# Turning the 32x32 blocks in VectorE's transposes instead of in ScalarE's copies, in a hybrid decoder trunk

## The chip, the cores and the metric

One core of a Trainium2 chip runs the whole program. The metric is the device time of one execution in microseconds; the kernel before takes 1524.26 us (median of 3 runs, 1524.03 to 1524.69).

## What is computed

Two layers over 512 prompt tokens and 64 sample tokens (8 sequences of 8) that share all weights: a pooling mixer and then a gated delta-net mixer, each followed by a SwiGLU feed-forward block, with RMS norms around each. All is float32. The part that matters here is the delta rule of the second mixer, cut to its core:

```python
kb = k * beta[..., None]
a_mat = jnp.where(strict, jnp.einsum('bhnid,bhnjd->bhnij', kb, k) * decay, 0.0)
t_mat = a_mat + jnp.eye(CHUNK, dtype=jnp.float32)
solve = functools.partial(lax.linalg.triangular_solve, left_side=True, lower=True,
                          unit_diagonal=True)
u = solve(t_mat, v * beta[..., None])
w = solve(t_mat, kb * jnp.exp(gc)[..., None])
```

Each head needs the inverse of unit triangular matrices `t_mat`. The kernel works with 128x128 matrices, of a head and a span of 128 tokens: 16 heads in 4 groups of 4, 4 spans, so 16 matrices a group.

## The kernel before, in words

**Stages.** The pooling mixer and the first feed-forward block come first, then the delta-net mixer (about 440 to 1000 us of the profile), then the second feed-forward block. Large products are made of three fp32r matmuls each (`mm3`): weights and activations are split into a rounded part and the rest (`wh`, `wl`, `hH`, `hL`), the rounded part by ScalarE, the rest by VectorE or GpSimd. Products of the delta rule on attention-like matrices are plain fp32 matmuls.

**The delta-net part.** It goes by groups of 4 heads. `project` makes the next group's projections (`ps_m` in PSUM, which ScalarE evicts to `u` or `zz`) and short convolutions (`ac`), while `core` (line 1845) does the delta rule of the present one. `core` writes the group's 16 matrices into `Uw` (128 partitions x 16 x 128), inverts their diagonal 32x32 blocks with `inv32` (line 1348), and then combines the blocks by matmuls (`ps_k<-T,Uw`, `ps_s<-Uw,Rs` and so on) with ScalarE copying results back into `Uw`.

**`inv32`.** Four blocks of 32 sit on the diagonal of each of the 16 matrices, so 64 blocks of 32x32 a group. Per quarter of the partitions, ScalarE copies the diagonal blocks out of `Uw` into the compact tile `D32`, half of the tile `ii` (a "front copy": 32 partitions x 16 matrices x 32 columns, 4 a group). In before the compact tile is ordered column first, matrix second, so that the copy writes contiguously 16 matrices' elements of one column and reads them 128 elements apart. VectorE transposes 32x32 squares of it into `A` (tile `ia`, 1024 elements a partition, each of them from `D32` repeated twice). 31 elimination steps follow, two VectorE operations each. Then VectorE transposes the result back into `D32`, and four more ScalarE copies (the "back copies") put it into the diagonal blocks of `Uw`, again with the order of the two inner dimensions turned. Names in the profile: `ii<-Uw` are the front copies, `ia<-ii` is the first transpose, `ii<-ii` the second (a STREAM_TRANSPOSE), `Uw<-ii` the back copies.

**The order of the work.** Nothing runs in the order in which it is written. Each call on an engine is recorded with a price (`Plan.cost`) and its dependences; `Plan.finish` then draws an order for all five queues by list scheduling with priorities, and refines the priorities window by window by numbers from a table, `CHOSEN`, that were found for this program beforehand. The order so drawn is what the chip gets; each engine takes its queue strictly in that order. The prices that matter here: ScalarE pays by the number of elements, VectorE's transpose by whether all its inner dimensions have step one ("flat"):

```python
        if eng == "ACT":
            extra = 93 * sum(self.is_ap(k.get(w)) for w in ("scale", "bias")) + (100 if "accum_out" in k else 0)
            t = 0.833 * max(n, 16) + (170 if ps else 205) + extra
            return t - 102, t
...
        if method == "transpose":
            flat = all(list(x.ap)[-1][0] == 1 for x in ins + [out])
            t = 1.27 * n + 50 if flat else 1.95 * n + 80
```

Where the planner leaves PE idle for long, it can put in a matmul of ones (`ps_w`) that fills the time. All instructions recorded this way carry one line in the profile, L471, so that rows are told apart by tile names. An element of a PSUM ring is reused only when its reader is done: `ps_m` has two banks, so a projection's matmuls wait when ScalarE is late with an eviction.

Of the kernel before, what the change touches and what calls it, by code (L numbers as in the profile page):

```python
# [20 lines left out]
P = 128  # L21
# [36 lines left out]
class Plan:  # L58
# [22 lines left out]
        "0: 1309 22695 62500 86149 76489 52345 11844 46362 86704 95002 35544 99175 66637 4282 17667 3769 58400 "  # L81
        "43626 61818 54108 98212 3351 36664 80504 27809 72224 29735 64917 23111 41727; 1: 49023 63007 16460 16433 "
        "48491 76138 74771 74114 65160 87426 17314 27044 28440 98688 51496 33718 593 1426; 2: 23373 59272 95208 "
        "89396 40366 27552 29680 19213 96021 18743 91102 85125 83403 91744 68462 45573 19331 18226 28408 16995 "
        "68187 22777 99797 41955 91122 61703; 3: 40396; 4: 67260 44319 57030; 5: 95301 46915 67764; 8: 83208 "
        "18345; 10: 99903 85569 22644 7666 75444 7917; 12: 59185 64395 62859 17333 99370 79611 45665 40125 66046; "
        "13: 94477 22197 77279 9674 64267 65493 96055 75041 73772 26094 59228 59668 29996 66590 85309; 14: 83042 "
        "12131 52755 11078 68435 7966 75550 43253 125 86835 85075 55755 62104 79190 42298 15154 45791; 15: 13478 "
        "99481 73642 25401 41010 41421 4472 94786 57263 70338 23457 86193 45351 1546 40 98196 4967 43483; 16: "
        "93817 89234 40602 94462 17450 57861 22756 50039 37491 70807 55020 62920 18061 28656 38897 47689 31571 "  # L90
        "48068 27422 61755 69394 54039 64619 42263 70100; 17: 33665 21486 9197 46860 52000 86161 59917; 18: 20924 "
        "43334 44329 81674 7114 17045 25962 66993 50082 96718 92807 12531 16023 18431 40440 24596 71944 21112 "
        "74829 68196 92347 31561 74253 3392 53332 92281 2151 99102; 19: 36174 31947 59659 69612 29455 87315 54537 "
        "65141 74338 82015 79392 19887 11167 92294 51046 68011 40758; 20: 97279 69020 2370 45304 28726 5480 85426 "
        "12019 40119 96999 10385 72026 34446 22404; 21: 70291 28702 739 31944 70903 1060 42873 31326 30516 12342 "
        "60990 51629 93117 93896 40802 48208 18456 19228 57064 4679 59610 21243 54322 22912 89277 28893 62715 "
        "60621 92572 61631; 22: 13485 22541 37816 52495 66992 95880 36259 78259 30823 9512 66230 80373; 23: 61483 "
        "44103 90015 42044 24735 32849 41632 1074 64956 20942 94616 72706 60830 42378 30741 90719 93544 81412 "
        "40715 53278 39455 89612 15442 43550 39219 57896 7747; 24: 25348 67719 13180 61748 88090 95516 85975 5084 "
        "92478 83615 56195 82259 69748 62427 65712 91857 26297 40732 78694 27404 53404 22318 67031 71586 6132; "  # L100
        "25: 76647 39712 2771 66343 14209 23210 97810 92132 78974 59399 25063 67858 21491 50489 62995 15236; 26: "
        "79626 36368 19214 80387 56401 35576 82717 60375 53873; 27: 21984 71594 50907 14377 32244 15901 41074 "
        "39715 28392 20799 74780 83699 61252 83397 7982 32598 99600 98403 4570 27483 22362 4823 2508; 28: 24551 "
        "98160 24793 94220 95277 24650 68875 45170 18708 59416 15825 86583 66687 11861 95570 58210 99313 97019; "
        "29: 85578 28888 61342 95415 75453 40719 32701 86064 81345 14893 68856 50949 85498 13575 51784 91952 "
        "27692 26008 40138 57302 3814 97612 4449 36357 22750 70909 28219 7818 28047; 30: 86054 60496 97999 69673 "
        "50610 25685 50210; 31: 74073 13115 29407 43294 58203 62386 60992 80895 97830 46726 88271 52280 70227 "
        "37935 45598 50679 82011 34563 64041 61743 56793 56266 28529 89658 56010 55213 38050 60174 94562 29310; "
        "32: 16887 16469 35631 32010 42196 69810 20338 57949 56793 9113 36835 10599 67930 73391 67445 89104 59334 "
        "10750 4354 31147 20157 21006 12454 24106 89881 81438 8886 66266 40719 99502; 33: 95295 91479 81844 39720 "  # L110
        "25951 85067 56132 25492 97663 47361 15928 80071 51459 54484 10833 17494 29033 31355 68865 10887 35990 "
        "5777 79080 89337 9764 76787; 34: 95089 63681 56199 59606 75724 79194 18810 42081 81189 51667 19488 51936 "
        "59115 4849 50732 93986 68335 96897 92514 31139 17828 30084 75477 789 82272 1621 74838 6441 14529 49710; "
        "35: 76201 60413 56949 82903 33174 54908 54426 49959 77520 99541 55443 56649 3401 80937 48261 52653 75001 "
        "63908 97280 79647 8351 98108 52226 14386 80233 7388 14686 29780; 36: 10839 81171 71314 53994 76242 86866 "
        "63984 70449 2577 95749 86944 93238 65312; 37: 33496 69024 75456 28597 71266 19980; 38: 24426 13066; 39: "
        "89400; 40: 42141; 41: 94909; 42: 72179; 43: 15012; 44: 19665 41475; 45: 90900 90312 85593; 47: 55533 "
        "59254 30957 68731; 48: 15838 ",
        "0: 25782 39795 26872 58963 96576 71590 57680 53529 3102 48534 72061 49705 6781 35832 91582 33069 50362 "
        "71108 33270 39184 13549 78972 45267 39225 2455 79100 17756 80269 12399 57409; 1: 46402 13382 59970 83415 "  # L120
        "14691 65163 44574 31472 34406 49161 12567 48273 66815 46533 18979; 2: 58040 13854 16950 54319 59560 "
        "16016 14965 7900 15237 90384 17027 79128; 3: 32401 47644 98719 63000 17976 69867 14151 42123 34927; 4: "
        "18661 97896 5163 42810 82890 14811 23796; 5: 6334 83049; 6: 6739; 7: 23073; 9: 27471 98644; 11: 78001; "
        "12: 34315 65271; 13: 23776 35070 5091 11421 17100 1203 8855; 14: 98971; 15: 61486 53284 63025 8383 6639 "
        "11331 62257 66892 82335 74223 26226 95867 59421; 16: 86166 76125 78281 27438 26729 41349 50987 18963 "
        "60114 75460 99525 42303 33029 86092 45319 53211 36241 77822 4554 51767 28255 52396 83151 21072 13812 "
        "92609 81561 50211 70654 98; 17: 23599 20302 3092 43937 52212 18247 56370 87394 16459 19578 8608 37160 "
        "57650 85260 31716 31832 97582 42879 62691 40643 31202 26562 64599 48393 14029 46348 44616 29960 88973 "
        "50291; 18: 30583 75810 48361 88631 26459 70970 52092 19211 31704 50319 80529 51246 71427 45060 25577 "
        "23134; 19: 31080 29136 81033 55723 40922 16359 72123 56616 2311 22281 53256 33100; 20: 44142 76207 5248 "  # L130
        "94534 38694 75978 77463 67624 7305 4227 3834 94400 7416 66904 14979 26203 48624 45889 78506 40677 47535 "
        "89571 39981 6928 87128 88968 66909 43851 4274 58642; 21: 69336 8122 99844 92973 38343 53747 20321 12346 "
        "73566 51737 18312 22680 63030 7717 62893 44178 2355 11057 30474 79072 92127 7792 27175 8540 346 80788 "
        "79335 3567 80360 81422; 22: 14406 26923 45288 92919 43118 28969 79433 6118 44420 22851 813 99007; 23: "
        "97983 9682 66931 43999 96699 423 69411 79350 45143 76896 41128 64696 85012 9854 72168 80918 49957 29132 "
        "1169 89269 99782 72655 91507 51767 73636 76975 16170 64069 39868 69735; 24: 87154 45026 32623 50533 "
        "21237 21939 85480 95525 86974 41709 70558 70996 80691 23737 73461 46677 88837 90458 70431 79576 54330 "
        "61929 56616 17684 89252 78294 53259 27624 24063 93374; 25: 35675 95804 41395 4068 11084 64995 49504 "
        "18653 58581 92762; 26: 24213 90088 97096 90603 49472 87352 45111 67548 52127 69154 64434 48680 76057 "
        "76606; 27: 46286 36048 17280 60605 32592 38247 90390 61321 7278 11649 34284 99813 84733 71233 16702 "  # L140
        "48885; 28: 5899 67480 92427 44895 55626 85677 83299 22128 68772 78982 44845 81471 43317 43522 79702 "
        "58206 29888 31552 50574 50128 99366 56292 67747; 29: 69130 12969 37521 72898 50292 65958 13013 28520 "
# [2035 lines left out]
```

## Time and profile before

| what | value |
|---|---|
| median of 3 runs | 1524.26 us |
| profiled execution | 1526.48 us, span 1524.8 us |
| PE busy | 1493.7 us, 98% |
| VectorE busy | 1126.6 us, 74% |
| ScalarE busy | 871.8 us, 57% |
| GpSimd busy | 107.6 us, 7% |
| mean granted TensorE clock | 0.997 |

The span runs from the first instruction's start to the last one's end. Busy time is the time in which an instruction of the engine runs; matmuls overlap, so a busy PE is not a PE at its peak, and idle time is the time between one instruction's end and the next one's start. A row of the timeline reads: start in us, duration in us, engine, line, operation, output<-inputs, shapes, count, and in brackets the idle time before it and what ended it. A row of the waits reads: who waited for whom, total us, times, the longest. A row of stretches reads: stretch, its length, then the busy time and count of PE, its weight loads, VectorE, ScalarE and GpSimd, the granted clock, the share of DMA and GB/s.

### The profile page before, as it was taken

Reading aid. Unit: us, or ns where it says so; the run is one execution under the profiler, and the core shown is the slowest. Engines: PE = TensorE matmul, PEld = TensorE weight load, DVE = VectorE, ACT = ScalarE, POOL = GpSimd, SP = SyncE. Lnnn points to the kernel's source line nnn. Section 1 sums busy time; section 2 is a strip of 40 time slices with the busy share of each in tenths; the row PEclk is TensorE's granted clock in tenths of the full one; section 3 lists DMA queues with packets and bytes.
Section 4 is the critical chain, followed back from the end, with each engine's and each line's share of the span. In section 5 each row is a group of like instructions: output and inputs, shape, how many; then the busy total and the mean of one; then the engine's idle time right before and its main releaser. Section 6 shows DMA issues by size and latency. Waiting matters only on the chain.

```text
span 1524.8 us, 30248 instructions
## 1 busy us (share of the span) xinstructions
PE 1493.7 (98%) x11782; PEld 1447.1 (95%) x11782; DVE 1126.6 (74%) x2277; ACT 871.8 (57%) x1842; POOL 107.6 (7%) x249
## 2 busy tenths in 40 slices
PE   8999999999999999999999999999999999999997
PEld 7999999999999898898899889899999999999997
DVE  6993575677788796995987798557796485767856
ACT  7753543435466866865785785546474453434545
POOL 4110000000011100200110110000020000000000
PEclk9999999999999999999999999999999999999999
DMA  7563323233467423434344433756864432233254
GB/s 190 155 185 114 94 77 108 67 109 96 138 180 207 117 82 97 134 102 128 102 121 115 125 112 105 210 164 190 249 204 143 134 95 86 78 94 111 69 166 135
DMA packets 344855, 197.86 MB, mean 130 GB/s; under 512 B 13500, under 2 KB 337693, under 8 KB 344704
## 3 DMA queue, kind: packets, MB, share of 16 engines
q1 hardware_dynamic: 344711, 195.92, 44.5%
q8 instruction: 93, 1.52, 0.4%
q14 instruction: 51, 0.41, 0.1%
HBM read 165.60 MB, written 30.52 MB: 129 GB/s over the span
## 4 chain that ended last, share of the span: by engine, by line
PE 83%; DVE 7%; ACT 5%; DMA 3%; issue 2%; POOL 0%; SPq 0%; ACTq 0%; DVEq 0%; POOLq 0%
PE ps_B L471 27%; PE ps_A L471 27%; PE ps_m L471 16%; PE ps_s L471 5%; PE ps_k L471 4%; PE ps_x L471 2%; DVE wl L471 1%; ACT Uw L471 1%; ACT ii L471 1%; PE ps_n L471 1%; ACT wh L471 1%; DVE ii L471 1%; PE ps_e L471 1%; DVE Uw L471 1%; DVE nacc L471 1%
## 5 line engine op out<-in xcount | busy, mean ns | idle before, releaser
L471 ACT ACTIVATE wh<-wraw 128x1024 fp32r<-128x1024 f32 (+4 forms) x239 | 232.5, 977 | 194.9 <-PE ps_B L471 65.3
L471 DVE TENSOR_TENSOR wl<-wraw,wh 128x1024 fp32r<-128x1024 f32 (+4 forms) x238 | 266.9, 1124 | 89.1 <-ACT wh L471 55.3
L471 PE MATMUL ps_m<-hH,wh 128*128 128x320 f32 (+1 forms) x832 | 251.7, 314 | 5.8 <-ACT u L471 5.1
L471 PE MATMUL ps_m<-hL,wh 128*128 128x320 f32 (+1 forms) x832 | 247.9, 309 | 0.0
L471 PE MATMUL ps_m<-hH,wl 128*128 128x320 f32 (+1 forms) x832 | 244.6, 308 | 0.0
L471 PEld LDWEIGHTS ps_m<-hH,wh 128*128 128x128 f32 x832 | 154.9, 189 | 10.6 <-ACT u L471 7.1
L471 PEld LDWEIGHTS ps_m<-hL,wh 128*128 128x128 f32 x832 | 154.8, 189 | 2.3 <-issue 0.8
L471 PEld LDWEIGHTS ps_m<-hH,wl 128*128 128x128 f32 x832 | 154.0, 189 | 1.8
L471 PE MATMUL ps_B<-hH,wh 128*128 128x320 f32 (+1 forms) x444 | 128.6, 304 | 0.1
L471 PE MATMUL ps_B<-hH,wl 128*128 128x320 f32 (+1 forms) x444 | 128.6, 304 | 0.1
L471 PE MATMUL ps_B<-hL,wh 128*128 128x320 f32 (+1 forms) x444 | 128.2, 303 | 0.0
L471 PE MATMUL ps_A<-hH,wh 128*128 128x256 f32 (+1 forms) x432 | 119.3, 290 | 0.6 <-ACT wh L471 0.6
L471 PE MATMUL ps_A<-hL,wh 128*128 128x256 f32 (+1 forms) x432 | 118.7, 289 | 0.0
L471 PE MATMUL ps_A<-hH,wl 128*128 128x256 f32 (+1 forms) x432 | 118.2, 289 | 0.0
L471 PE MATMUL ps_A<-aH,wl 128*128 128x288 f32 (+2 forms) x408 | 111.7, 296 | 0.0
L471 PE MATMUL ps_A<-aL,wh 128*128 128x288 f32 (+2 forms) x408 | 111.2, 296 | 0.0
L471 PE MATMUL ps_A<-aH,wh 128*128 128x288 f32 (+2 forms) x408 | 111.1, 296 | 0.0
L471 PE MATMUL ps_B<-aH,wh 128*128 128x288 f32 x296 | 84.0, 297 | 0.0
L471 PE MATMUL ps_B<-aH,wl 128*128 128x288 f32 x296 | 83.5, 296 | 0.1
L471 PE MATMUL ps_B<-aL,wh 128*128 128x288 f32 x296 | 83.1, 295 | 0.0
L471 PEld LDWEIGHTS ps_B<-hH,wh 128*128 128x128 f32 x444 | 81.9, 188 | 0.8 <-ACT nsq L471 0.4
L471 PEld LDWEIGHTS ps_B<-hH,wl 128*128 128x128 f32 x444 | 81.9, 188 | 0.7 <-DVE wl L471 0.4
(458 smaller groups left out, 3996.6 us busy)
## 6 DMA issues: line engine op xcount, KB each, us to landing
wraw<-in_ffn_w_in_dram SPq DMA_DIRECT2D x77, 512.0 KB
wraw<-in_gdn_w_in_dram SPq DMA_DIRECT2D x56, 512.0 KB
graw<-in_ffn_w_in_dram SPq DMA_DIRECT2D x33, 512.0 KB
wraw<-in_ffn_w_out_dram SPq DMA_DIRECT2D x32, 448.0 KB
wraw<-in_gdn_w_out_dram SPq DMA_DIRECT2D x24, 512.0 KB
wraw<-in_ffn_w_out_dram SPq DMA_DIRECT2D x32, 320.0 KB
St<-in_state_gdn_rec_dram SPq DMA_DIRECT2D x32, 256.0 KB
out_dram<-St SPq DMA_DIRECT2D x32, 256.0 KB
```

Source lines behind the costliest of these rows:

```text
L471: calls[e](*a, **k)
```

## The change

The compact tile takes the order of the big tile: matrix first, column second. ScalarE's eight copies a group then walk both sides in runs of 32 contiguous elements. The turning round is done by VectorE's two transposes: the first reads `D32` with a step of 32 elements, the second writes it with such a step (it read with a step of 16 before and does so still). The arithmetic is the same. As the prices of the recorded calls differ (the first transpose is no longer flat), the table `CHOSEN` was found anew, four strings as before, and the whole order is drawn anew.

```diff
     CHOSEN = (
-        "0: 1309 22695 62500 86149 76489 52345 11844 46362 86704 95002 35544 99175 66637 4282 17667 3769 58400 "
...
+        "0: 7936 55843 86527 33991 97722 31117 8629 9687 47150 83676 16297 15132 53952 77128 31040 66847 59628 "
...
         XT = ap_.tile([P, 2, 512], F32, name="ii", tag="ii", bufs=1)
         X = XT[:, 0].rearrange("p (j i) -> p j i", j=32)
-        D32 = XT[:, 1].rearrange("p (i h) -> p i h", h=16)
+        D32 = XT[:, 1].rearrange("p (h i) -> p h i", h=16)
         for b in range(4):
             s = slice(32 * b, 32 * b + 32)
-            ACT.activation(D32[s], W[s, :, s].rearrange("p h i -> p i h"), AF.Copy)
-        DVE.transpose(A, D32.unsqueeze(2).to_broadcast([P, 32, 2, 16]))
+            ACT.activation(D32[s], W[s, :, s], AF.Copy)
+        DVE.transpose(A, D32.rearrange("p h i -> p i h").unsqueeze(2).to_broadcast([P, 32, 2, 16]))
...
-        DVE.transpose(XT[:, 1].rearrange("p (i j) -> p i j", j=32), X.rearrange("p j i -> p i j"))
+        DVE.transpose(D32.rearrange("p h (i d) -> p i d h", d=2), X.rearrange("p j i -> p i j"))
         for b in range(4):
             s = slice(32 * b, 32 * b + 32)
-            ACT.activation(W[s, :, s].rearrange("p h i -> p i h"), D32[s], AF.Copy)
+            ACT.activation(W[s, :, s], D32[s], AF.Copy)
             yield 0.6
```

In the built program the rest of the instructions stay the same in kind and nearly in number: on PE 17 filling matmuls become 21, on ScalarE 29 loads of function tables become 26, and some 20 small operations that VectorE or GpSimd may do change sides. The places in the order that matter for the prediction are shown here, ScalarE's queue ahead of the second group's inverse. Before:

```order
L471 ACTIVATE QD<-QD,ngs 128x128 x3
L471 ACTIVATE u<-ps_m 128x256
L471 ACTIVATE wh<-wraw 128x1024
L471 ACTIVATE ac<-u,cwt 128x600
L471 ACTIVATE ii<-Uw 32x512 x4
L471 ACTIVATE u<-ps_m 128x256
L471 ACTIVATE u<-ps_m 128x8x8
L471 ACTIVATE des<-ps_s 64x128 x2
```

And in the change (`oss` are the norms of the group before, `des` the samples' decays):

```order
L478 ACTIVATE u<-ps_m 128x256
L478 ACTIVATE u<-ps_m 128x8x8
L478 ACT_TABLE_LOAD
L478 ACTIVATE oss<-oss,epsd 128x20
L478 ACTIVATE ii<-Uw 32x512 x4
L478 ACTIVATE wh<-wraw 128x1024
L478 ACTIVATE u<-ps_m 128x256
L478 ACT_TABLE_LOAD
```

A rounding of weights, `wh`, has moved from ahead of the four copies to between them and the next eviction. The second place is PE's queue ahead of the same group's return from the inverse (`nct` is turned for the convolution's state, `sn` is the samples' inverse). Before:

```order
L471 MATMUL ps_x<-ident,nct 27x128 x2
L471 MATMUL ps_m<-hH,wh 128x320
L471 MATMUL ps_m<-hL,wh 128x320
L471 MATMUL ps_x<-ident,nct 27x128
L471 MATMUL ps_m<-hH,wl 128x320
L471 MATMUL ps_x<-ident,nct 27x128
L471 MATMUL ps_m<-hH,wh 128x320
```

And in the change:

```order
L478 MATMUL ps_m<-hH,wl 128x320
L478 MATMUL ps_x<-ident,nct 27x128 x4
L478 MATMUL ps_k<-sn 128x128
L478 MATMUL ps_m<-hH,wh 128x320
L478 MATMUL ps_m<-hL,wh 128x320
```

Plain-fp32 transposes that stood one by one between fp32r matmuls stand in one run of four.

285 rows, old and new, of the table CHOSEN are left out of this document.

## The prediction

> **What bounds the kernel now.** I read the page's first part, then the stretches, then PE's waits, and last the tile that the change touches.
>
> ```profile
> PE 1493.7 (98%) x11782; PEld 1447.1 (95%) x11782; DVE 1126.6 (74%) x2277; ACT 871.8 (57%) x1842; POOL 107.6 (7%) x249
> ...
> 200.00:240.00 40.00, 40.00 (x302) 39.84 (x301) 24.76 (x42) 17.61 (x27) 0.00 (x0) 1.00 0.27 76
> ...
> 440.00:1000.00 560.00, 542.29 (x4668) 507.79 (x4666) 450.56 (x1110) 384.57 (x990) 63.56 (x146) 1.00 0.46 130
> ```
>
> TensorE (PE) is the bound. In the feed-forward stretches (200 to 240) it is never idle, and nothing on ScalarE or VectorE can matter there. In the delta-net part, from 440 to 1000, PE is idle for 560 - 542.29 = 17.7 us. That is all the room this change has, unless it alters PE's own work. Who ends that idle time stands in PE's waits:
>
> ```profile
> PE ps_m L471 <- ACT u L471: 5.1, 4, 1.7
> ...
> PE ps_k L471 <- ACT Uw L471: 1.7, 3, 0.8
> ```
>
> The longest wait of all is for an eviction by ScalarE, four times, and there are four inverses (`inv32`, one a group). The tile `ii` of the inverse shows what its steps cost (minimum/median/maximum in ns), and the last two rows, of `T` and `ac`, give contiguous neighbours:
>
> ```profile
> L471 ACT ACTIVATE ii<-Uw x16: 1060/1120/1171, 542.5 to 907.9; 32x512 f32<-32x512 f32 x16
> L471 ACT ACTIVATE Uw<-ii x16: 1062/1119/1162, 581.1 to 947.2; 32x512 f32<-32x512 f32 x16
> ...
> L471 DVE STREAM_TRANSPOSE ia<-ii x4: 1245/1245/1246, 548.4 to 909.0; 128x1024 f32<-128x1024 f32 x4
> L471 DVE STREAM_TRANSPOSE ii<-ii x4: 1071/1082/1084, 580.0 to 941.3; 128x512 f32<-128x512 f32 x4
> ...
> L471 DVE STREAM_TRANSPOSE T<-Uw x12: 690/701/703, 582.2 to 952.3; 32x512 f32<-32x512 f32 x12
> ...
> L471 ACT ACTIVATE ac<-ac x16: 614/632/653, 526.1 to 949.7; 128x512 f32<-128x512 f32 x16
> ```
>
> A copy of 512 elements that walks one side out of order takes 1.12 us; an activation of 512 elements in order takes 0.63. The planner's price for either is 0.833 x 512 + 205 = 632 ns (its cost rule for ACT looks at the number of elements only), so the order of before was drawn as if four copies took half of what they take. The trace of the second group, first ScalarE and VectorE, then PE, shows what that does ahead of an inverse:
>
> ```profile
> 654.90 4.51 ACT L471 ACTIVATE ii<-Uw 32x512 f32<-32x512 f32 x4
> 659.43 0.50 ACT L471 ACTIVATE u<-ps_m 128x256 f32<-128x256 f32 x2
> ...
> 659.44 1.25 DVE L471 STREAM_TRANSPOSE ia<-ii 128x1024 f32<-128x1024 f32 x1 [1.53 <-ACT ii L471]
> ...
> 658.03 0.28 PE L471 MATMUL ps_m<-hH,wl 128*128 128x256 f32 x1
> 658.14 0.28 PE L471 MATMUL ps_m<-hH,wh 128*128 128x256 f32 x1
> 659.98 0.41 PE L471 MATMUL ps_m<-hH,wh 128*128 128x320 f32 x1 [1.56 <-ACT u L471]
> ```
>
> Four copies hold ScalarE from 654.90 to 659.41; only then does it empty the PSUM bank that the projection's next `ps_m` needs. PE, which steps every 0.11 to 0.12 us, loses 659.98 - 658.14 - 0.12 = 1.72 us here: the idle 1.56, and 0.16 of drained pipeline that the idle column doesn't count.
>
> **The change, part by part.** *Front copies (16, four a group).* They become an in-order write and reads in runs of 32. Bounds: 0.63 us each by the `ac` row, 1.12 if the jump after every 32 elements costs as much as now. I take 0.63, since 31 of 32 steps are contiguous: four take about 2.5 us in place of 4.51, 2.0 less. The waits that stand right behind front copies are these and the one of 659.98:
>
> ```profile
> 549.03 0.33 PE L471 MATMUL ps_x<-ident,ac 128*128 128x128 f32 x1 [1.25 <-ACT ac L471]
> ...
> 785.00 0.39 PE L471 MATMUL ps_m<-hH,wh 128*128 128x256 f32 x1 [1.47 <-ACT u L471]
> ...
> 909.40 0.38 PE L471 MATMUL ps_m<-hH,wh 128*128 128x256 f32 x1 [1.72 <-ACT u L471]
> ```
>
> 1.25 + 1.56 + 1.47 + 1.72 = 6.0 us, each shorter than the 2.0 that the copies give back: -6.0. In the second group's queue, as the section on the change shows it, the eviction now also stands behind a `wh`, which spends part of what the copies gave back; but this time the order was drawn at a price that the copies keep.
>
> *Back copies (16).* Also -2.0 us a group. Waits behind them:
>
> ```profile
> 583.77 0.38 PE L471 MATMUL ps_m<-hH,wh 128*128 128x256 f32 x1 [0.33 <-ACT u L471]
> ...
> 586.02 0.25 PE L471 MATMUL ps_k<-T,Uw 128*64 128x32 f32 x2 [0.45 <-ACT Uw L471]
> ...
> 701.34 0.33 PE L471 MATMUL ps_x<-ident,vt 128*128 128x128 f32 x1 [0.50 <-ACT nco L471]
> ...
> 827.23 0.24 PE L471 MATMUL ps_k<-T,Uw 128*64 128x32 f32 x1 [0.45 <-ACT Uw L471]
> ...
> 828.32 0.30 PE L471 MATMUL ps_k<-T,Uw 128*64 128x32 f32 x3 [0.79 <-ACT Uw L471]
> ...
> 948.77 0.38 PE L471 MATMUL ps_k<-sn 128*128 128x128 f32 x1 [1.09 <-ACT sn L471]
> ...
> 705.09 1.22 DVE L471 TENSOR_TENSOR wl<-wraw,wh 128x1024 fp32r<-128x1024 f32 x1 [3.67 <-ACT wh L471]
> 706.35 0.75 DVE L471 SCALAR_TENSOR_TENSOR vt<-ps_x,prm,vt 128x512 f32<-128x512 f32 x1
> ...
> 707.15 0.33 PE L471 MATMUL ps_x<-ident,vt 128*128 128x128 f32 x1 [1.13 <-DVE vt L471]
> ```
>
> The last one is a copy's too: `wh` stood behind the copies, VectorE waited 3.67 us for it with `vt` queued behind, and PE for `vt`. Together 0.33 + 0.45 + 0.50 + 0.45 + 0.79 + 1.09 + 1.13 = 4.7 us. I take 3.7, leaving 1.0 for a second transpose that may be dearer. With 0.16 of drain for some ten waits that go, -1.6 more.
>
> *First transpose (4).* Its read now steps 32 elements. From the rows: in order, (1245 - 701)/512 = 1.06 ns an element over 0.16 us fixed; with a stepped read (`ii<-ii`), (1082 - 160)/512 = 1.80. So 0.16 + 1024 x 1.80 = 2.0 us, 0.76 more each, 3.0 in all; the lower bound is nothing, if the doubled read hides it. It lies in the inverse's chain, where the front copies give 2.0 back, and the planner now prices it at 1.95 x 1024 + 80 = 2077 ns: nothing on PE; without that cover, 3.0.
>
> *Second transpose (4).* Its read was stepped already; now the write steps as well. Bounds: 1.08 if the slower side sets the time, 1.08 + (1.08 - 0.70) = 1.46 if the two add, 1.5 us in four. I take 1.08, the row of the same read; that is also the planner's price. [...] No run shows a write that steps on VectorE so far.
>
> *The order.* The planner's numbers are new, so every queue is drawn anew. One change of PE's order can be counted: from plain-fp32 to fp32r matmuls it goes 415 times before, 381 times after. The two pieces of PE's order above show how: singles became runs. What a run saves:
>
> ```profile
> 533.33 1.03 PE L471 MATMUL ps_k<-qk 128*128 128x256 f32 x4
> 534.01 0.50 PE L471 MATMUL ps_m<-hH,wl 128*128 128x320 f32 x1
> 534.34 0.28 PE L471 MATMUL ps_m<-hL,wh 128*128 128x256 f32 x1
> ...
> 539.54 0.62 PE L471 MATMUL ps_k<-qk 128*128 128x256 f32 x2
> 539.81 0.49 PE L471 MATMUL ps_m<-hH,wh 128*128 128x320 f32 x1
> 540.14 0.31 PE L471 MATMUL ps_m<-hL,wh 128*128 128x320 f32 x1
> ```
>
> Two records (one product) and the matmul behind them take 540.14 - 539.54 = 0.60 us, four and the matmul 1.01; less 0.15 for that matmul's own step, 0.45 against 0.86, so joining two saves 0.04. 34 x 0.04 = 1.4 at most; for transposes it is less, so -0.7. Against that, four more of the planner's filling matmuls (`ps_w`, 17 to 21), about 0.2 us each where they fill nothing: +0.9.
>
> *Sum:* -6.0 - 3.7 - 1.6 - 0.7 + 0.9 = -11.1. The 17.7 - 10.7 = 7 us of idle time that no copy causes is drawn anew too; I give 1.1 back for it, a choice, and it may be 3 either way. That makes -10: the profiled execution, 1526.5 us (span 1524.8 and 1.7 around it), would be 1516.5; against the median of 1524.3, 1514.3.
>
> **Rivals.** *The waits move (0.16).* With the eviction behind a `wh` of 0.98 us, it comes 2.5 + 0.98 = 3.5 us after the copies start, against 4.5: 1.0 less, not 2.0, and 0.6 of the 1.56 stays. If half of all copy waits survive so, or others take their place, -3 to -5: about 1520. For it: ScalarE's queue of the second group. Against it: the new prices are true.
>
> *VectorE becomes the bound, and it is slower (0.08).*
>
> ```profile
> 640.00:680.00 40.00, 38.16 (x281) 37.21 (x280) 36.63 (x97) 28.76 (x55) 6.62 (x15) 1.00 0.41 118
> 680.00:720.00 40.00, 38.37 (x424) 36.49 (x423) 24.82 (x63) 22.44 (x46) 2.91 (x7) 0.96 0.44 124
> ```
>
> Around an inverse VectorE is busy 36.63 of 40 us. The transposes add 0.76 to 0.76 + 0.38 = 1.14 us a group there, in front of `wl`, `QD` and the inverse's own steps, for which PE waits in the end. It decides once this exceeds VectorE's idle 3.4 us or falls where none is left; then all 4.6 us reach PE, while the old waits return under VectorE's name: 1524.3 + 4.6 - 0.7 + 0.9 = 1529. Against it: 1.14 is a third of 3.4.
>
> *The change doesn't do what it says (0.06).* The jump after each run, not the turned order, makes the copy slow; it stays at 1.12 us, the transposes add 3.0 to 4.6, part of it on the chain: 1524 to 1528.
>
> **The numbers.** Forecast 0.70, rivals 0.16, 0.08 and 0.06. Low end: all 10.7 and 1.8 of drain, 1.4 of joined runs and 3 of luck, less nothing, is -17: 1507. It also takes in that the granted clock of 0.96 (680 to 720, worth 0.04 x 40 = 1.6 us) may not come back. High end: the moved waits, 1522; past it lie the last two rivals and a little of each tail, 0.2. A measurement of this kernel tells about 0.2%, 3 us, from no change: faster 0.70 + 0.13 of the first rival = 0.83; same 0.03 + half of the last and a rest = 0.09; slower 0.08.
>
> **What would show it.** Right: `ii<-Uw` and `Uw<-ii` at 0.6 us; `ia<-ii` near 2.0; PE's waits for `ACT u` and `ACT Uw` around the four inverses gone; PE's idle time from 440 to 1000 near 8 us. Wrong: copies at 1.1; or copies at 0.6 and the same idle under other names, VectorE's among them.

## The result, and the profile after

The change takes 1513.43 us (median of 4 runs, 1512.39 to 1514.92) against 1524.47 for the kernel before on the same chip: a ratio of 0.9916, 95% interval 0.9894 to 0.9938, so 9 to 16 us faster. (The ratio is not the quotient of the two medians, which are 11.0 us apart; that is 0.9928 and lies inside the interval.) Measured again beside the last experiments the ratio was 0.9908 (0.9888 to 0.9928). The forecast was 1514.3, in a range of 1507 to 1522.

The profiled execution takes 1514.92 us with a span of 1513.2, 11.6 less than before. PE's busy time went from 1493.7 to 1492.4, its idle time from 31.1 to 20.8: 10.3 of the 11.6 us are idle time that is gone. First the page's busy times:

```profile
PE 1492.4 (99%) x11790; PEld 1445.6 (96%) x11790; DVE 1130.1 (75%) x2280; ACT 852.2 (56%) x1839; POOL 112.1 (7%) x246
```

and the delta-net stretch, whose second figure is PE's busy time:

```profile
440.00:1000.00 560.00, 551.39 (x4750) 516.23 (x4749) 460.49 (x1129) 370.45 (x1002) 65.26 (x140) 1.00 0.47 133
```

PE is idle for 560 - 551.39 = 8.6 us of that stretch, 17.7 before: 9.1 of the 10.3 us come from there. The steps of the inverse, by the tile `ii` (minimum/median/maximum, ns):

```profile
L478 ACT ACTIVATE ii<-Uw x16: 614/628/632, 544.5 to 902.9; 32x512 f32<-32x512 f32 x16
L478 ACT ACTIVATE Uw<-ii x16: 613/628/632, 583.6 to 943.1; 32x512 f32<-32x512 f32 x16
...
L478 DVE STREAM_TRANSPOSE ia<-ii x4: 2052/2073/2099, 547.8 to 904.2; 128x1024 f32<-128x1024 f32 x4
L478 DVE STREAM_TRANSPOSE ii<-ii x4: 1159/1172/1185, 582.4 to 939.3; 128x512 f32<-128x512 f32 x4
```

The copies went from 1.12 to 0.63 us, the first transpose from 1.25 to 2.07, the second from 1.08 to 1.17. ScalarE gives back 32 x 0.49 = 16 us, VectorE pays 4 x (0.83 + 0.09) = 3.7. ScalarE's queue at the second group's inverse:

```profile
652.78 2.55 ACT L478 ACTIVATE ii<-Uw 32x512 f32<-32x512 f32 x4 [1.61 <-DVE Uw L478]
655.35 1.06 ACT L478 ACTIVATE wh<-wraw 128x1024 fp32r<-128x1024 f32 x1
656.32 0.37 ACT L478 ACTIVATE u<-ps_m 128x256 f32<-128x256 f32 x1
```

Four copies take 2.55 us, where they took 4.51; the eviction behind `wh` starts 3.5 us after the first copy. And who ends PE's waits now, from 440 on:

```profile
PE ps_x L478 <- DVE vt L478: 3.4, 5, 1.5
PE ps_s L478 <- DVE rv L478: 1.2, 1, 1.2
PE ps_x L478 <- DMA crow<-in_state_gdn_conv_dram: 1.2, 1, 1.2
PE ps_x L478 <- ACT nco L478: 1.0, 2, 0.7
PE ps_k L478 <- DVE QD L478: 0.6, 2, 0.4
```

The waits for `ACT u` (5.1 us), `ACT ac` (1.2), `ACT Uw` (1.7) and `ACT sn` (1.1) have left the list. What leads it now is `vt`, a product on VectorE, and that is partly a transfer: at 710.17 VectorE itself had waited 3.14 us for the DMA that reads `z_d` into `vt`.

### The profile page after: what moved, and what is told of

The parts are those of the page before. It is cut to its first block, busy times and chain, and to the rows that moved or that the text cites. A ratio compares the mean times of both kernels' runs of the same rounds, so it can differ in the third digit from the quotient of the medians.

```text
span 1513.2 us, 30277 instructions
## 1 busy us (share of the span) xinstructions
PE 1492.4 (99%) x11790; PEld 1445.6 (96%) x11790; DVE 1130.1 (75%) x2280; ACT 852.2 (56%) x1839; POOL 112.1 (7%) x246
## 3 DMA queue, kind: packets, MB, share of 16 engines
q8 instruction: 93, 1.52, 0.4%
## 4 chain that ended last, share of the span: by engine, by line
PE 57%; DVE 4%; ACT 2%; DMA 2%; issue 1%; SPq 0%; ACTq 0%; DVEq 0%
PE ps_m L478 16%; PE ps_A L478 15%; PE ps_B L478 14%; PE ps_s L478 5%; PE ps_k L478 4%; PE ps_x L478 2%; DVE vt L478 1%; DVE ac L478 1%; PE ps_n L478 1%; DMA vt<-z_d 1%; DVE wl L478 1%; DVE ii L478 0%; DMA out_dram<-St 0%; ACT wh L478 0%; DMA og<-og_d 0%
## 5 line engine op out<-in xcount | busy, mean ns | idle before, releaser
L478 PE MATMUL ps_m<-hH,wh 128*128 128x320 f32 (+1 forms) x832 | 246.9, 311 | 0.3 <-ACT zz L478 0.3
```

The costliest lines, as they stand in the source:

```text
L478: calls[e](*a, **k)
```

## The experiments

The theory: PE waits because four stepped copies hold ScalarE 2 us longer than four copies in order, ahead of each inverse and behind it. The rivals: the gain comes from the new table, not from the copies; the harm was the planner's wrong price of the copies, not their length; VectorE becomes the bound. Gains in us are one minus the ratio, times the median of before on the same chip (1527.6 to 1528.4). The expected times below count from a before of 1524.3, so it is the gains that can be compared.

### One order, two inverses: the change's copies in the order of before

The new `inv32` in the kernel before, with its table; the planner is told to price the first transpose as flat, so that it draws the same order, row for row.

```diff
-            flat = all(list(x.ap)[-1][0] == 1 for x in ins + [out])
+            flat = n == 1024 or all(list(x.ap)[-1][0] == 1 for x in ins + [out])
...
+        D32 = XT[:, 1].rearrange("p (h i) -> p h i", h=16)
...
+            ACT.activation(D32[s], W[s, :, s], AF.Copy)
```

> The turned inverse (copies in order, transposes with steps) in the order of before, row for row on every engine. Theory (the slow copies made PE wait): the waits for ACT u, ACT ac and ACT Uw around the four inverses go, 6.0 us ahead and 3.7 to 4.7 behind, with some 1.6 of drain: 1513 to 1515.5. Rival (the new table drew a better order, and the copies' time was hidden): within 2 us of before, 1522 to 1526. VectorE as the bound: slower than before by up to 4 us.

Measured: ratio 0.9929 (0.9904 to 0.9955), 10.9 us faster than before (7 to 15); median 1516.79 against 1528.43, which this chip gives for before. That is the theory's figure: 1513 to 1515.5 is 9 to 11 us below 1524.3. With the order fixed, and the number of instructions on every engine the same, nothing but the inverse's own instructions can have done this. The stretch:

```profile
440.00:1000.00 560.00, 550.52 (x4741) 516.78 (x4740) 459.40 (x1121) 374.81 (x1000) 64.56 (x146) 1.00 0.47 133
```

and PE's waits from 540 on:

```profile
PE ps_x L471 <- DVE vt L471: 3.0, 4, 1.2
PE ps_k L471 <- DVE QD L471: 1.6, 3, 0.7
...
PE ps_k L471 <- DVE sn L471: 0.4, 1, 0.4
PE ps_k L471 <- DVE BD L471: 0.4, 1, 0.4
```

Idle time falls from 17.7 to 9.5 us; no wait for `ACT u`, `ACT ac` or `ACT Uw` is left. Two small ones on VectorE are new, `sn` and `BD`, whose instructions stand some way behind the first transpose in its queue. Not all of the relief was kept: from 540 on, PE's waits for ScalarE fell from 10.4 to 0.2 us, but those for VectorE rose from 3.9 to 6.5, about a quarter of what had gone. One wait that I had put down to the copies came back in another form, as VectorE's queue shows:

```profile
701.38 0.75 DVE L471 SCALAR_TENSOR_TENSOR vt<-ps_x,prm,vt 128x512 f32<-128x512 f32 x1 [0.27 <-DMA vt<-z_d]
...
708.69 0.75 DVE L471 SCALAR_TENSOR_TENSOR vt<-ps_x,prm,vt 128x512 f32<-128x512 f32 x1 [4.95 <-DMA vt<-z_d]
```

The first `vt` comes 5 us sooner than before (706.35), but the next one then waits 4.95 us for its transfer, and PE, at 709.49, 1.19 us for it.

### One inverse, two orders: the old copies in the order of the change

The reverse: the old `inv32` in the change, with `n != 1024 and` in the same price.

> The inverse of before (copies of 1.12 us, transposes of 1.25 and 1.08) in the order of the change. Theory: the copies are 2 us a group late ahead of the inverse and 2 us behind it, less 0.9 us that the transposes give back, so the waits come back, under ACT's name: 1520 to 1525. Rival (order alone): within 2 us of the change, 1511.5 to 1515.5.

Measured: 0.9972 (0.9954 to 0.9990), 4.3 us faster than before (1.5 to 7). Counted from 1524.3 that is 1520, the fast end of the 1520 to 1525 expected. PE's waits:

```profile
PE ps_m L478 <- ACT u L478: 4.1, 3, 1.7
...
PE ps_x L478 <- ACT ac L478: 1.5, 1, 1.5
PE ps_x L478 <- ACT nco L478: 1.3, 1, 1.3
PE ps_k L478 <- ACT Uw L478: 1.2, 2, 0.8
```

and the stretch:

```profile
440.00:1000.00 560.00, 546.06 (x4705) 510.83 (x4704) 456.29 (x1125) 382.90 (x998) 62.43 (x139) 1.00 0.46 131
```

The waits for ScalarE are back, and PE is idle for 13.9 us. So the turned inverse carries most of the gain, and the order adds a little: 4.3 us with the old copies, and about 2 to 3 with the new ones (0.9929 against 0.9916 and 0.9908, whose intervals overlap, so that this second figure is not clear of noise).

### The front alone, and the back alone

In the order of before, the turned layout is used for the copies out and the first transpose only, or for the second transpose and the copies back only.

```diff
+        D32n = XT[:, 1].rearrange("p (h i) -> p h i", h=16)
...
-            ACT.activation(D32[s], W[s, :, s].rearrange("p h i -> p i h"), AF.Copy)
+            ACT.activation(D32n[s], W[s, :, s], AF.Copy)
```

> Order of before; only the front half is turned (copies out of the big tile and the first transpose), the back half is that of before. Theory: the four waits of 6.0 us ahead of the inverses go with 0.6 of drain, and the inverse ends 1.2 us earlier (2.0 less 0.8), which may take something off the waits behind it: 1515 to 1518. Rival (order alone): 1522 to 1526.

> Order of before; only the back half is turned (second transpose and copies back). Theory: the waits of 6.0 us ahead of the inverses stay, 3 to 4.7 us behind them go: 1519 to 1522; together with the front-only kernel the two gains add up to about that of both. Rival (order alone): 1522 to 1526.

Measured: front alone 0.9954 (0.9937 to 0.9970), 7.0 us faster; back alone 0.9959 (0.9939 to 0.9980), 6.3 us faster, more than the 2 to 5 expected of it, though the interval (3 to 9) takes those in. Both sum to 13.3, against 10.9 (7 to 15) for the two together: additive within what the runs can tell. The waits say it more sharply. The front alone:

```profile
PE ps_k L471 <- ACT Uw L471: 1.7, 3, 0.8
...
PE ps_k L471 <- ACT sn L471: 1.1, 1, 1.1
```

and the back alone:

```profile
PE ps_m L471 <- ACT u L471: 4.8, 3, 1.7
...
PE ps_x L471 <- ACT ac L471: 1.2, 1, 1.2
```

Each half leaves the other half's waits for ScalarE: 1.7 and 1.1 are those of before behind the inverses, 4.8 + 1.2 = 6.0 those ahead of them. PE's waits for VectorE from 540 on are 5.9 us with the front alone and 4.1 with the back alone, 3.9 before: what came back under VectorE's name came with the front half.

### VectorE's side of the bill: the first transpose twice

In the change, each first transpose is issued twice.

```diff
                 calls[e](*a, **k)
+                if ops[i][9] == "transpose" and e == "DVE" and self.size(a[0]) == 1024:
+                    calls[e](*a, **k)
```

> The change, its order kept, with the first transpose of each inverse done twice in a row (the second time for nothing): 2.07 us more on VectorE and in the inverse's chain, 4 times, 8.3 us in all. Theory (PE waits only where something comes later than the order was drawn for): part of it comes through, 2 to 6 us over the change, as waits behind the inverses. VectorE as the bound: all 8.3 us or more. If the chain has slack everywhere: less than 2 us.

Measured: 0.9954 of before (0.9937 to 0.9971), against 0.9916 and 0.9908 for the change: 6 to 7 us of the 8.1 that the second transposes take come through by the ratios, whose intervals allow anything from 2 to 11. The medians, 1521.71 against 1513.43 and 1513.62, differ by 8.1 to 8.3. That is more than the 2 to 6 expected of the theory, and it does not tell "most of it" from "all of it". New in PE's waits:

```profile
PE ps_k L478 <- DVE BD L478: 1.6, 1, 1.6
PE ps_k L478 <- DVE ks L478: 1.4, 1, 1.4
PE ps_m L478 <- ACT u L478: 1.4, 1, 1.4
PE ps_x L478 <- ACT ac L478: 1.2, 1, 1.2
```

There is one in each group, 5.7 us in all. `BD` and `ks` stand right behind the transpose in VectorE's queue; `u` and `ac` are ScalarE's, which in these two groups had itself waited longer for VectorE (3.14 us for `ac` at 665.71, 1.94 for `BD` at 793.37, where it was 1.01 and 1.05 in the change). So the place of the transpose has little cover: of the 8.1 us more put there, 5.7 reach PE by these waits, and all of them by the medians. What the transpose's own 0.83 us more cost is a different question, which this run doesn't answer; it only makes it doubtful that it cost nothing.

### Was it the price? Three orders without the table

The table is emptied in before (first), in before with a true price for stepped copies (second), and in the change (third).

```diff
-    CHOSEN = (
...
+    CHOSEN = ()
...
             t = 0.833 * max(n, 16) + (170 if ps else 205) + extra
+            if not ps and list(out.ap)[0][1] == 32 and any(list(x.ap)[-1][0] > 4 for x in ins + [out]):
+                t += 0.954 * n
```

> The kernel before with an empty table CHOSEN, so with the order that the planner draws without refinement. It says what the table is worth: 10 to 30 us slower than before. It is the measure for the next two.

> The kernel before with an empty table, and the planner told the true price of the stepped copies (0.954 ns an element more, so 1.12 us). If the wrong price was the harm (PE's work could have covered the copies, had the order known): near the change without a table, within 3 us, so 5 to 10 us faster than before without a table. If the copies' time itself is the harm: within 3 us of before without a table.

> The change with an empty table. If the gain is the copies', not the new table's: 6 to 12 us faster than before without a table. If the gain came with the new table: within 3 us of it.

Measured: 1566.99, 1567.59 and 1551.89 us; ratios to before 1.0253 (1.0224 to 1.0283), 1.0246 (1.0220 to 1.0273), 1.0148 (1.0124 to 1.0171). The table is worth some 39 us, more than the 10 to 30 expected. The true price gains nothing that can be measured, the short copies gain 15.1 us, more than the 6 to 12 expected. Part of that may be the granted clock's, whose mean over the runs was 0.9925, 0.9912 and 0.9978. By what the last section shows, an estimate at equal clock is 11 to 14 us for the short copies and 1 to 2 for the true price. The page of before without a table:

```profile
PE 1526.9 (98%) x11986; PEld 1475.7 (94%) x11986; DVE 1134.2 (72%) x2283; ACT 875.8 (56%) x1844; POOL 103.8 (7%) x243
```

its filling matmuls (two records each):

```profile
L326 PE MATMUL ps_w<-ones x238: 270/275/582, 1.3 to 1555.1; 128*128 128x128 f32 x119
```

and one of PE's waits from 540 on:

```profile
PE ps_m L330 <- ACT u L330: 3.4, 3, 1.7
```

The page with the true price:

```profile
PE 1532.0 (98%) x12000; PEld 1478.8 (94%) x12000; DVE 1134.4 (72%) x2285; ACT 877.2 (56%) x1844; POOL 103.6 (7%) x241
```

its filling matmuls:

```profile
L328 PE MATMUL ps_w<-ones x252: 270/275/582, 1.3 to 1555.9; 128*128 128x128 f32 x126
```

and the longest of its waits:

```profile
PE ps_k L332 <- DVE QD L332: 5.2, 6, 2.4
PE ps_x L332 <- DVE vt L332: 3.9, 3, 2.1
```

With the true price `ps_m` hardly waits for `ACT u` any more (0.2 us), and PE is idle for 34.7 us in place of 38.9. But PE is busy 5.1 us longer: 14 more records of filling matmuls make 2.1 us of it (36.15 against 34.05), and where the rest comes from was not followed (this execution's granted clock was lower, 0.993 against 0.995). One reading is that the planner, knowing that the copies are slow, has too little to put in their place; that is not shown beyond the fillers. Each of these is one draw of an order, so that a few us between them may be luck; the gap to the short copies is not explained by the price. A table found anew for before at its true price was not tried, so what refinement could make of that price stays open.

### Letting the evictions through

Before's order, but the third and fourth front copy stand behind the next `u` or `ac` on ScalarE, where one comes before the transpose.

```diff
+                if e == "ACT" and out == "ii":
+                    copies += 1
+                    if copies % 4 in (3, 0):
+                        held.append((calls[e], a, k))
+                        continue
...
                 calls[e](*a, **k)
+                if e == "ACT" and out in ("u", "ac"):
+                    for f, aa, kk in held:
+                        f(*aa, **kk)
+                    held = []
```

> The kernel before, its slow copies and its order kept, except that the third and fourth front copy of each inverse stand behind the next eviction (u) or activation (ac) on ScalarE; that takes effect in three of the four groups (in the third group no eviction comes before the transpose). The inverse starts 0.4 to 0.6 us later, the evictions 2.2 us earlier. Theory (PE waits because what it needs stands behind slow copies in ScalarE's queue): the waits of 1.25, 1.56 and 1.72 us go, that of 1.47 stays; 3 to 5 us faster than before. Rival (the length of the inverse's chain is what counts): within 1 us of before or slower by up to 2.

Measured: 1.0011 (0.9992 to 1.0029), no gain. The 3 to 5 us that the theory expected did not come. It is the rival's figure, but only partly for its reason. PE's waits:

```profile
PE ps_m L482 <- ACT u L482: 3.8, 4, 1.7
PE ps_k L482 <- DVE BD L482: 2.6, 2, 1.5
```

and VectorE at the first group's inverse:

```profile
548.08 1.25 DVE L482 STREAM_TRANSPOSE ia<-ii 128x1024 f32<-128x1024 f32 x1 [2.21 <-ACT ii L485]
549.36 0.29 DVE L482 TENSOR_TENSOR ks<-ps_k,ks 64x128 fp32r<-64x128 f32 x1
```

In the first and the fourth group the wait for ScalarE went, or shrank from 1.72 to 0.29 us, and one for `BD` on VectorE came, 1.52 and 1.03 us: `BD` stands behind the transpose, and the transpose waits for the last copy. In the second group the edit missed: only the larger part of the bank's eviction was let through, the smaller one still stood behind the copies, and the wait stayed (1.69 us, 1.56 before). In the third the edit changed nothing, as expected. So the theory of ScalarE's queue alone was too narrow: the slow copies hold two queues, ScalarE's and, through the transpose, VectorE's. In the two groups where one was let through, PE waited for the other.

### Sharing the copies with VectorE

In the change's order, every second back copy, or every second back and front copy, is done by VectorE; beside them the change itself.

```diff
+                if (out, src) in (("Uw", "ii"),):
+                    half += 1
+                    if half % 2:
+                        self.vector.tensor_copy(a[0], a[1])
+                        continue
```

> The change, its order kept, with every second back copy done by VectorE in place of ScalarE (8 of 16). ScalarE's queue gets 1.25 us a group shorter, VectorE's 0.5 to 0.9 us longer. If PE's remaining waits behind the inverses are for ScalarE's copies: 1 to 3 us faster than the change. If they are for VectorE's queue (vt): 0 to 3 us slower.

> As the kernel before this one, and every second front copy on VectorE too (16 of 32 in all). Ahead of the inverse the change has no wait left for ScalarE, so nothing to gain there; VectorE's queue gets 0.5 to 0.9 us a group longer in front of the inverse: 0 to 4 us slower than the kernel with the back half alone.

> The change itself, on the same chip as the kernels beside it, for their comparison: 0.9916 of before, as measured, within 0.9894 to 0.9938.

Measured: back half 0.9900 (0.9880 to 0.9920), median 1512.37; both halves 0.9922 (0.9904 to 0.9941), 1515.88; the change 0.9908 (0.9888 to 0.9928), 1513.62. A VectorE copy of the same block takes less than ScalarE's:

```profile
L486 ACT ACTIVATE Uw<-ii x8: 625/627/627, 581.7 to 938.9; 32x512 f32<-32x512 f32 x8
L484 DVE COPY Uw<-ii x8: 391/416/418, 581.7 to 940.3; 32x512 f32<-32x512 f32 x8
```

The back half's 1.2 us over the change, and the loss of 2.3 with both halves, go the way that was expected, but the intervals overlap: against the change neither is settled. Between the two, every run with the back half alone (1512.13 to 1512.58) was faster than every run with both (1513.75 to 1516.64), as expected.

## Why the prediction was right, point by point

**Front copies, -6.0 and some drain.** Right: the four waits are gone in the change, and the front alone measures 7.0 us (5 to 10). The price of 0.63 us was right too (0.628). The drain was not measured by itself.

**Back copies, -3.7 of 4.7.** Right in sum (6.3, 3 to 9, with the drain), wrong in one part: the wait of 1.13 us for `vt` was not simply a copy's. `vt` did come sooner (at 701.38 us with the turned inverse in the old order, at 706.35 before), and the next `vt` waited 4.95 us for a transfer in its place.

**First transpose, 2.0 us.** Measured 2.07. The cover that the prediction counted on was there: in the old order the first group's transpose ends at 548.68 us, 1.0 sooner than before (549.65), though it takes longer. The doubtful step is "nothing on PE". Of a second transpose in that place most seems to have come through, and in the old order two waits of 0.4 us each appeared further back in VectorE's queue. What the dearer transpose alone cost stays open. The copies' relief is larger than this, so the sign didn't hang on it.

**Second transpose, 1.08.** Measured 1.17, of bounds 1.08 and 1.46. The write that now steps cost 0.09 us over the same read before it, a quarter of the 0.38 between the bounds: in this transpose the two sides did not add in full, and the row that I took was 0.09 short.

**The order, +1.3.** The sign was wrong: joined runs, fillers and "other waits drawn anew" were put at -0.7 + 0.9 + 1.1. The order alone measures -4.3 (1.5 to 7 faster) with the old copies, and about -2 to -3, not clear of noise, with the new ones. What in it gains was not separated.

**The total.** The inverse's share was near: -11.3 forecast, -10.9 measured. That the time came within 1 us of the forecast is partly luck. The order's miss of some 3 to 6 us should have shown; but the four runs of before beside the result had a median of 1524.47, where 1527.6 to 1528.4 were measured on the chips of the experiments, and by the ratio the gain is 12.8 us, not 10 or 11.

**The reason.** I leaned on the price: the copies hurt because the order was drawn for copies half as long. The three orders without a table speak against this as the whole cause: with the stepped copies at their true price the time is the same within noise (1567.59 us against 1566.99), and only short copies bring the gain (1551.89). What the runs show in its place is the length itself, 1.12 us a copy against 0.63: the copies stand in ScalarE's queue ahead of evictions and, through the transpose, in VectorE's ahead of what PE needs next.

**The rivals.** The waits did not move to `wh`, though `wh` stands there: PE's list from 440 on has neither `u` nor `wh`. VectorE as the bound was the right place to look, and some waits did come back under its name (6.5 us from 540 on with the turned inverse in the old order, 3.9 before), but far too few to make the kernel slower. The copies became as short as forecast (0.628 us).

## What to carry to other kernels

Where an engine of strict order is nearly always busy (here PE, 98%), look at what ends its few waits, and ask which queue the slow instruction holds: here 16 us less on an engine that is busy 57% of the time were worth 11 us, because most of some eleven short waits ended behind it. A layout should be turned by the instruction that pays least for it: a step cost 0.49 us on each of eight copies, and 0.83 and 0.09 on two transposes. And a true price in a planner need not buy back the time: here, without a table, it gained nothing that could be measured.

## What the runs showed of the hardware that was not expected

The granted TensorE clock differed between two executions in their first 60 us. The first two stretches of the back-alone kernel, whose profiled execution took 1530.0 us against a median of 1520.4:

```profile
0.00:30.00 30.00, 24.90 (x158) 23.17 (x158) 19.23 (x54) 22.73 (x51) 16.15 (x74) 0.83 0.78 214
30.00:60.00 30.00, 29.84 (x147) 27.15 (x146) 18.30 (x50) 17.22 (x48) 4.16 (x6) 0.66 0.27 79
```

and of the front-alone kernel, whose order is the same:

```profile
0.00:30.00 30.00, 24.84 (x165) 23.07 (x166) 19.88 (x57) 23.60 (x55) 16.04 (x74) 0.89 0.85 215
30.00:60.00 30.00, 29.85 (x221) 27.78 (x221) 25.98 (x75) 22.81 (x59) 5.25 (x7) 1.00 0.46 132
```

Between 30 and 60 us PE gets through 147 matmuls at a clock of 0.66, and 221 at 1.00. The first group's copy of `eye` into `ii`, ahead of the inverse and the same in both kernels, starts at 541.9 us in the one and at 531.0 in the other: the whole 10 us are lost before the part that differs. Time and clock go together over many runs as well: in the 61 runs of before beside the experiments, 0.001 less of an execution's mean granted clock goes with about 1 us more (correlation -0.8). The comparison on which the cause rests is hardly touched: before and the turned inverse in its order had nearly the same mean clock (0.9936 and 0.9940). In the others before's mean was mostly 0.001 to 0.004 lower, so that some of those gains may be the clock's: an estimate is 2 of the change's 14 us beside the last experiments (0.9939 and 0.9960) and 1.5 of the order's 4.3. What decides the clock was not tried.
